# Retention into GLU on one core: one store issued from ScalarE, one gelu moved behind a value projection, operand splits given other predecessors

## The chip, the cores and the metric

The kernel runs on one core of a Trainium2 chip. The metric is the device time of one execution in microseconds, as a median over runs. TensorE (PE) does the matrix products, VectorE (DVE), ScalarE (ACT) and GpSimd (POOL) the elementwise work, and transfers are issued from SyncE's queue (SP) and from ScalarE's queue.

## What is computed

The program is a two-layer trunk over 1024 frames of width 1024, in float32. Only layer 0 matters here, and of it the join of two branches:

```python
# branch A: state-space layer, then a gated linear unit
y = jax.nn.gelu(y)
y = y * jax.nn.sigmoid(y @ glu_w + glu_b)          # (1024 x 1024) @ (1024 x 1024)
# branch B: retention, 8 heads, in chunks
scores = einsum('bnihd,bnjhd->bnhij', q, k) * intra   # the mask
out = scores @ v + cross                               # then a norm per head
# join
x = x + concat([y * silu(g_s5), out * silu(g_ret)]) @ w_out
```

Layer 1 (projections, a causal convolution of width 31, a norm and an output projection) follows and is the same in both kernels.

## The kernel before

**Products.** Every float32 weight and operand is split into a high and a low part (`h`, `l` in tile names: `wh_`/`wl_` for weights, `y11h`/`y11l` for operands), and each product is three matmuls of 512 columns: L200 (high by high), L201 (weight high by operand low), L202 (weight low by operand high). A weight block of 512 KB is loaded from SP into one of three `wf` buffers, ACT makes the high part (L189), and POOL or DVE the low part (L190).

**Stages.** Layer 0 runs the input projections beside the state-space layer, then `retention` with four pairs of heads (0 to 3), then the gated linear unit (GLU), then the output projection `mm_wo`. In each pair TensorE projects k (`mm_k`), q (`mm_q`) and the values (`mm_v`, eight blocks of 128 frames, each copied out by ACT at L1115 as `v`). Then it transposes k (`ktp`), makes the states (`kv`, summed by DVE into `S` at L1185), the scores (`sp`) and the outputs (`ro`). The scores are copied and masked by DVE into `sc` (L1198), twice for each half of the frames; `self.masked[0]` and `self.masked[1]` are the last of these for each half. The outputs are normalised (BN_STATS L1235, `rs` L475 on ACT, `on` L1241), turned (`rt`, L1249) and multiplied with the gate (`grl`, L1252).

**The GLU's operand.** While retention runs, `y_pass(k)` makes the operand of the GLU from y (rows k and k+4 of eight blocks). It loads y into `yp`, applies gelu on ACT (L958, tiles `yn_0` to `yn_7`), stores the result to DRAM (`yn_d`, L960), and then has DVE combine the two tiles in place (L966 to L969; the first of them overwrites half of the second tile and so needs its store done). The combinations are split (`th` L973, low part L974) and stored (`t_d`). The `yp` buffer is single: the two loads and the two `th` tiles of a pair use it in turn, so the second `th` needs the first one's store done.

**The GLU.** Its product is done with seven quarter-size products in place of eight. The first two quarters of y, `y11` and `y21`, come from `yn_d` by `load_split`: a load into a `wf` buffer (SP, L1284), a high part on ACT (L1260), a low part on DVE (L1262). The quarter products are `mm_glu1x` (x = 0 to 3: weight blocks `glu0` with `y11` and `glu1` with `y21` for x = 0 and 1, `glu2` and `glu3` for x = 2 and 3), then `mm_glu6x` (operand `yt2`, weights `glu4` and `glu5`) and so on. Their PSUM buffers are three in rotation: `mm_glu13` takes the one that `mm_glu10` had, once ACT has read it by the tanh `sg0` (L1337), and that stands behind the last `rs` of retention.

**What sets the order.** The program is handed to a scheduler that orders each engine's instructions by priorities and a simulated time line; each engine then runs its own list in order. `tc.issue_after(ins)` tells it not to place an instruction before another. `load_split` has two such hooks, `cast` for the high parts and `behind` for the low parts:

```python
def split(self, src, hi, lo, eng, behind=None, cast=None):
    with self.tc.issue_after(cast.ins) if cast else nullcontext():
        self.nc.scalar.copy(hi[:], src)
    with self.tc.issue_after(behind.ins) if behind else nullcontext():
        return eng.tensor_tensor(lo[:], src, hi[:].bitcast(F32), op=ALU.subtract)
```

`self.third_v` is the copy of the third value block of a pair and `self.last_v` that of the eighth. `self.last_kt` is the last copy of the transposed keys (L1158).

Of the kernel before, what the change touches and what calls it, by code (L numbers as in the profile page):

```python
# [19 lines left out]
P = 128  # L20
# [21 lines left out]
def mv(ap):  # L42

    return ap.rearrange("p (a c) -> p c a", a=LANES)


def un(ap):

    return ap.rearrange("p (c a) -> p a c", a=LANES)


def nat(ap):

    return ap.rearrange("p (a c) -> p a c", a=LANES)
# [16 lines left out]
class Trunk:  # L71
# [875 lines left out]
    def y_pass(self, rp, k):  # L947


        nc = self.nc  # L950
        yns = []
        for i, cb in enumerate((k, k + 4)):
            yt = rp.tile([P, 8, P], F32, name=f"yp_{cb}", tag="yp", bufs=1)
            nc.sync.dma_start(yt[:], self.y_d[cb].rearrange("i h g m -> (h g) i m"))
            yn = rp.tile([P, P, 8], F32, name=f"yn_{cb}", tag="ynt", bufs=2)

            with self.tc.issue_after((self.last_v if i else self.third_v).ins) if k == 2 else nullcontext():
                nc.scalar.activation(yn[:], yt[:].rearrange("p i m -> p m i"), AF.Gelu_apprx_tanh)  # L958
            yn = yn[:].rearrange("p m i -> p (m i)")
            nc.sync.dma_start(self.yn_d[cb * P:(cb + 1) * P], yn)  # L960
            yns.append(yn)
        (b11, b12), (b21, b22) = ((y[:, :HALF], y[:, HALF:]) for y in yns)
        v = nc.vector
        yield
        with self.tc.issue_after(self.last_raw.ins):
            v.tensor_tensor(b22, b22, b12, op=ALU.subtract)  # L966
            v.tensor_tensor(b12, b12, b11, op=ALU.subtract)
            v.tensor_tensor(b11, b22, b11, op=ALU.add)
            v.tensor_tensor(b21, b11, b21, op=ALU.subtract)  # L969
        yield  # L970
        for i in range(2):
            hi = rp.tile([P, T], F32R, name=f"th{i}_{k}", tag="yp", bufs=1)
            v.tensor_copy(hi[:], yns[i])  # L973
            v.tensor_tensor(yns[i].bitcast(F32R), yns[i], hi[:].bitcast(F32), op=ALU.subtract)  # L974
            nc.sync.dma_start(self.t_d[i, 0, k * P:(k + 1) * P], hi[:].bitcast(F32))
            nc.sync.dma_start(self.t_d[i, 1, k * P:(k + 1) * P], yns[i])
# [121 lines left out]
    def ret_values(self, pair):  # L1098

        nc = self.nc  # L1100
        wv = [self.wnext(f"v{pair}_{i}") for i in range(2)]
        vt = self.rp.tile([P, 8, 256], F32, name=f"v_{pair}", tag="v", bufs=2)
        for b in range(8):
            ps = self.bank(f"mm_v{pair}_{b}", aux=False)
            h, o = b // 4, (b % 4) * P
            for kb in range(KB):
                xh, xl = self.xs[h][kb]
                i, k4 = kb // 4, kb % 4
                wh = wv[i][0][:].rearrange("p (k a) n -> p k (a n)", a=2)[:, k4, :]
                wl = wv[i][1][:].rearrange("p (k a) n -> p k (a n)", a=2)[:, k4, :]  # L1110
                wh, wl = mv(wh), mv(wl)
                nc.tensor.matmul(ps[:, :256], xh[:, o:o + P], wh, start=kb == 0, stop=False)
                nc.tensor.matmul(ps[:, :256], xh[:, o:o + P], wl, start=False, stop=False)
                nc.tensor.matmul(ps[:, :256], xl[:, o:o + P], wh, start=False, stop=kb == KB - 1)
            self.last_v = nc.scalar.mul(nat(vt[:, b, :]), un(ps[:, :256]), self.Rtok[:, b:b + 1])  # L1115
            if b == 2:
                self.third_v = self.last_v
        return lambda p, b, hh: vt[:, b, hh * P:(hh + 1) * P]

    def ret_values_wide(self):  # L1120
# [143 lines left out]
    def layer0_back_and_layer1(self, st):  # L1264
        nc, A = self.nc, self.A
# [8 lines left out]
        def load_split(parts, name, h, wide, behind=None, cast=None):  # L1274

            res = []
            for i, part in enumerate(parts):
                if wide:
                    if i % 2 == 0:
                        f2 = self.wp.tile([P, 2, HALF], F32, name=f"{name}f{i}", tag="wf", bufs=3)  # L1280
                    f = f2[:, i % 2, :]
                else:
                    f = lp.tile([P, HALF], F32, name=f"{name}f{i}", tag="tp", bufs=3)[:]
                nc.sync.dma_start(f, part)  # L1284
                a, b = (self.op_tile(self.opA, f"A{h}", f"{name}{q}{i}") for q in "hl")
                self.split(f, a, b, v, behind, cast)
                res.append((a, b))
            return res
# [5 lines left out]
        B = lambda j, h: [self.yn_d[rows(4 * j + k), hs(h)] for k in range(4)]  # L1294
# [8 lines left out]
                res.append(ops)  # L1303
            return res

        b11, b21 = load_split(B(0, 0), "y11", 0, True, None, self.last_v), load_split(B(1, 0), "y21", 0, True, self.last_kt, self.last_v)
        ys = [[None] * KB for _ in range(2)]

        u2 = [lp.tile([P, HALF], F32, name=f"gu2_{n}", tag=tag, bufs=1) for n, tag in enumerate(("cq", "cs", "pilot", "sq"))]
# [618 lines left out]
```

## Time and profile before

| | us |
|---|---|
| median of 3 runs | 1147.6 (1144.61 to 1149.13) |
| span of the profiled execution | 1149.0 |
| PE busy | 1125.3 (98%) |
| DVE busy | 847.4 (74%) |
| POOL busy | 654.3 (57%) |
| ACT busy | 489.5 (43%) |
| mean granted TensorE clock | 0.991 |

The page gives the profiled execution's span and no other time of it; the span lies among the three runs. Matmuls overlap, and a busy PE in this table is not a PE at its peak. TensorE stands still for about 24 us in all, and an instruction of any engine waits for the ones ahead of it in the same engine's list.

### The profile page before, as it was taken

Reading aid. Unit: us, or ns where it says so; the run is one execution under the profiler, and the core shown is the slowest. Engines: PE = TensorE matmul, PEld = TensorE weight load, DVE = VectorE, ACT = ScalarE, POOL = GpSimd, SP = SyncE. Lnnn points to the kernel's source line nnn. Section 1 sums busy time; section 2 is a strip of 40 time slices with the busy share of each in tenths; the row PEclk is TensorE's granted clock in tenths of the full one; section 3 lists DMA queues with packets and bytes.
Section 4 is the critical chain, followed back from the end, with each engine's and each line's share of the span. In section 5 each row is a group of like instructions: output and inputs, shape, how many; then the busy total and the mean of one; then the engine's idle time right before and its main releaser. Section 6 shows DMA issues by size and latency. Waiting matters only on the chain.

```text
span 1149.0 us, 17198 instructions
## 1 busy us (share of the span) xinstructions
PE 1125.3 (98%) x6286; PEld 986.1 (86%) x6286; DVE 847.4 (74%) x1464; ACT 489.5 (43%) x719; POOL 654.3 (57%) x448
## 2 busy tenths in 40 slices
PE   9999999999999999989899999999999999999997
PEld 7888878888888889889788888888888888888787
DVE  6975788887418469484669622599999889999844
ACT  6423222333223231322446523555545677444674
POOL 2059999999246354232476011489544568677663
PEclk9999999999999999989899999999999999999999
DMA  9344445556388766858999988665778755357865
GB/s 352 111 134 154 122 164 177 179 174 206 114 279 290 241 220 186 292 171 304 348 382 308 342 287 282 185 240 202 239 256 293 242 188 175 119 182 257 287 226 193
DMA packets 117636, 261.45 MB, mean 228 GB/s; under 512 B 10672, under 2 KB 42288, under 8 KB 116912
## 3 DMA queue, kind: packets, MB, share of 16 engines
q1 hardware_dynamic: 114096, 247.78, 64.1%
q10 hardware_dynamic: 3456, 12.58, 2.9%
q8 instruction: 49, 0.80, 0.3%
q14 instruction: 35, 0.29, 0.1%
HBM read 181.48 MB, written 74.65 MB: 223 GB/s over the span
## 4 chain that ended last, share of the span: by engine, by line
PE 74%; DVE 13%; DMA 5%; issue 3%; POOL 3%; ACT 2%; SPq 0%; POOLq 0%; DVEq 0%; ACTq 0%
DVE cv L1535 5%; PE mm_wo L201 5%; PE mm_wo L200 5%; PE mm_wo L202 5%; PE mm_g L200 4%; PE mm_g L201 4%; PE mm_g L202 4%; PE mm_b L201 2%; PE mm_b L202 2%; PE mm_b L200 2%; PE mm_a L202 2%; PE mm_a L201 2%; PE mm_a L200 2%; PE mm_u L202 2%; PE mm_u L200 2%
## 5 line engine op out<-in xcount | busy, mean ns | idle before, releaser
L1535 DVE SCALAR_TENSOR_TENSOR cv<-u,convw,cv 128x512 f32<-128x512 f32 x398 | 273.0, 748 | 6.8 <-ACT cv L1514 4.8
L1508 POOL TENSOR_TENSOR tp<-tp,tp 128x512 f32<-128x512 f32 x64 | 82.9, 1296 | 33.9 <-ACT tp L1507 32.8
L200 PE MATMUL mm_g<-xh,wh_g 128*128 128x512 f32 x256 | 99.4, 388 | 0.0
L201 PE MATMUL mm_g<-xl,wh_g 128*128 128x512 f32 x256 | 98.1, 383 | 0.0
L202 PE MATMUL mm_g<-xh,wl_g 128*128 128x512 f32 x256 | 97.9, 382 | 0.0
L437 POOL TENSOR_TENSOR s1q<-s1q,s1q 128x512 f32<-128x512 f32 x12 | 17.1, 1427 | 81.4 <-ACT s1q L432 81.4
L1507 ACT ACTIVATE tp<-u,convw 128x512 f32<-128x512 f32 x64 | 45.4, 719 | 35.6 <-POOL tp L1508 34.8
L200 PEld LDWEIGHTS mm_g<-xh,wh_g 128*128 128x128 f32 x256 | 48.8, 191 | 8.7 <-issue 1.2
L202 PEld LDWEIGHTS mm_g<-xh,wl_g 128*128 128x128 f32 x256 | 48.8, 191 | 7.1
L201 PEld LDWEIGHTS mm_g<-xl,wh_g 128*128 128x128 f32 x256 | 48.7, 190 | 6.9 <-issue 0.4
L190 POOL TENSOR_TENSOR wl_v<-wf_v,wh_v 128x1024 fp32r<-128x1024 f32 x12 | 31.0, 2590 | 38.0 <-ACT wh_v L189 38.0
L190 POOL TENSOR_TENSOR wl_glu<-wf_glu,wh_glu 128x1024 fp32r<-128x1024 f32 x14 | 35.1, 2506 | 30.7 <-ACT wh_glu L189 30.7
L202 PE MATMUL mm_oc<-zh,wl_woc 128*128 128x512 f32 (+1 forms) x144 | 51.0, 357 | 0.3 <-DMA wl_woc<-lo_woc 0.3
L201 PE MATMUL mm_oc<-zl,wh_woc 128*128 128x512 f32 (+1 forms) x144 | 51.1, 356 | 0.0
L200 PE MATMUL mm_oc<-zh,wh_woc 128*128 128x512 f32 (+1 forms) x144 | 50.7, 363 | 0.0
L201 PE MATMUL mm_u<-xl,wh_u 128*128 128x512 f32 x128 | 48.5, 381 | 0.7 <-DVE xl L316 0.7
L200 PE MATMUL mm_wo<-ysh,wh_wos 128*128 128x512 f32 x128 | 48.9, 382 | 0.0
L200 PE MATMUL mm_g<-h1h,wh_cg 128*128 128x512 f32 x128 | 48.9, 382 | 0.0
L201 PE MATMUL mm_b<-h1l,wh_cb 128*128 128x512 f32 x128 | 48.7, 381 | 0.1
L202 PE MATMUL mm_b<-h1h,wl_cb 128*128 128x512 f32 x128 | 48.6, 380 | 0.0
L201 PE MATMUL mm_wo<-ysl,wh_wos 128*128 128x512 f32 x128 | 48.5, 379 | 0.0
L202 PE MATMUL mm_wo<-ysh,wl_wos 128*128 128x512 f32 x128 | 48.5, 379 | 0.0
(526 smaller groups left out, 3613.3 us busy)
## 6 DMA issues: line engine op xcount, KB each, us to landing
wf_g<-w_ab SPq DMA_DIRECT2D x16, 512.0 KB
wf_wos<-w_out SPq DMA_DIRECT2D x16, 512.0 KB
wf_wor<-w_out SPq DMA_DIRECT2D x16, 512.0 KB
wf_cb<-w_c SPq DMA_DIRECT2D x16, 512.0 KB
wf_ca<-w_c SPq DMA_DIRECT2D x16, 512.0 KB
wf_woc<-w_out_c SPq DMA_DIRECT2D x16, 512.0 KB
wf_v<-w_v SPq DMA_DIRECT2D x12, 512.0 KB
wf_cg<-w_c SPq DMA_DIRECT2D x11, 512.0 KB
```

What stands on the lines that cost most here:

```text
L190: self.low_made = lo[i].tensor_tensor(wl[:].rearrange(fl)[:, c], wf[:, c], h.bitcast(F32), op=ALU.subtract)
L200: nc.tensor.matmul(ps, wh[:, kb, :], xh, start=start, stop=False, **more)
L201: nc.tensor.matmul(ps, wh[:, kb, :], xl, start=False, stop=False, **more)
L202: self.last_mm = nc.tensor.matmul(ps, wl[:, kb, :], xh, start=False, stop=stop, **more)
L437: nc.gpsimd.tensor_tensor(a, a, sq[:], op=ALU.add)
L1507: nc.scalar.mul(sk[:], u[:, k:k + HALF], cw[:, nb, k:k + 1])
L1508: gp.tensor_tensor(s0[:], s0[:], sk[:], op=ALU.add)
L1535: v.scalar_tensor_tensor(dst[:], *tap, accs_[i][:], op0=ALU.mult, op1=ALU.add)
```

## The change

Four edits, all at the end of retention:

1. The store of `yn_6` (pair 2, second tile) is issued from ACT's queue in place of SP's.
2. The gelu of `yn_7` (pair 3, second tile) is placed behind the third value block of pair 3.
3. The high parts of `y11` are placed behind the sixth value block of pair 3 in place of the eighth.
4. The low parts of `y21` are placed behind the last masks of pair 3 in place of the last copy of the transposed keys.

```diff
-            with self.tc.issue_after((self.last_v if i else self.third_v).ins) if k == 2 else nullcontext():
+            behind = {(2, 0): self.third_v, (2, 1): self.last_v, (3, 1): self.third_v}.get((k, i)) if k > 1 else None
+            with self.tc.issue_after(behind.ins) if behind else nullcontext():
                 nc.scalar.activation(yn[:], yt[:].rearrange("p i m -> p m i"), AF.Gelu_apprx_tanh)
             yn = yn[:].rearrange("p m i -> p (m i)")
-            nc.sync.dma_start(self.yn_d[cb * P:(cb + 1) * P], yn)
+            (nc.scalar if (k, i) == (2, 1) else nc.sync).dma_start(self.yn_d[cb * P:(cb + 1) * P], yn)
...
             if b == 2:
                 self.third_v = self.last_v
+            elif b == 5:
+                self.late_v = self.last_v
...
-        b11, b21 = load_split(B(0, 0), "y11", 0, True, None, self.last_v), load_split(B(1, 0), "y21", 0, True, self.last_kt, self.last_v)
+        b11, b21 = load_split(B(0, 0), "y11", 0, True, None, self.late_v), load_split(B(1, 0), "y21", 0, True, self.masked[1], self.last_v)
```

No instruction is added or removed. Every engine's list is the same up to the end of pair 2's values and again from the first few blocks of `mm_wo` on; between them the scheduler moved more than the four edits name. In the changed kernel a line of the functions below `y_pass` has a number one to three higher.

ACT, at the end of pair 2's values (`rs_4` is pair 2's first norm). Before:

```order
L958 ACTIVATE yn_6_4620<-yp_6_4618 128x1024
L189 CAST wh_v3_0_4843<-wf_v3_0_4842 128x1024
L475 ACT_TABLE_LOAD
L475 ACTIVATE rs_4_0_4720<-mv_4_0_4711,epst_78 128x4
L475 ACTIVATE rs_5_0_4738<-mv_5_0_4729,epst_78 128x4
```

Now:

```order
L959 ACTIVATE yn_6_4620<-yp_6_4618 128x1024
L189 CAST wh_v3_0_4843<-wf_v3_0_4842 128x1024
L961 DMA yn_d_89<-yn_6_4620 128x1024
L475 ACT_TABLE_LOAD
L475 ACTIVATE rs_4_0_4720<-mv_4_0_4711,epst_78 128x4
```

The store now stands on ACT behind the gelu and one cast. On SP it stood behind the two loads of the gate (`grl_4`, `grl_5`) and ahead of two weight loads, which all stay there.

DVE, around the masks of pair 3. Before:

```order
L1262 TENSOR_TENSOR y21l0_5471<-y21f0_5468,y21h0_5470 128x512
L1185 SCALAR_TENSOR_TENSOR S_3_5246<-S_3_5246,g128_3202,kv1_3_5260 128x128
L1262 TENSOR_TENSOR y21l1_5476<-y21f0_5468,y21h1_5475 128x512
L1185 SCALAR_TENSOR_TENSOR S_3_5246<-S_3_5246,g128_3202,kv1_3_5260 128x128 x2
L1262 TENSOR_TENSOR y21l2_5482<-y21f2_5479,y21h2_5481 128x512
L1262 TENSOR_TENSOR y21l3_5487<-y21f2_5479,y21h3_5486 128x512
L1198 TENSOR_TENSOR sc0_3_5270<-sp10_3_5284,retmask_3_4836 128x512
L1198 TENSOR_TENSOR sc1_3_5271<-sp11_3_5285,retmask_3_4836 128x512
L1235 BN_STATS st_6_0_5316<-ro0_6_5300 128x6 x4
```

Now:

```order
L1188 SCALAR_TENSOR_TENSOR S_3_5246<-S_3_5246,g128_3202,kv1_3_5260 128x128
L1201 TENSOR_TENSOR sc1_3_5271<-sp01_3_5273,retmask_3_4836 128x512
L1201 TENSOR_TENSOR sc0_3_5270<-sp10_3_5284,retmask_3_4836 128x512
L1201 TENSOR_TENSOR sc1_3_5271<-sp11_3_5285,retmask_3_4836 128x512
L1265 TENSOR_TENSOR y21l0_5471<-y21f0_5468,y21h0_5470 128x512
L1265 TENSOR_TENSOR y21l1_5476<-y21f0_5468,y21h1_5475 128x512
L1265 TENSOR_TENSOR y21l2_5482<-y21f2_5479,y21h2_5481 128x512
L1265 TENSOR_TENSOR y21l3_5487<-y21f2_5479,y21h3_5486 128x512
L1238 BN_STATS st_6_0_5316<-ro0_6_5300 128x6 x4
```

The states and masks no longer have the low parts of `y21` between them; the low parts now stand ahead of retention's statistics.

ACT and SP, at the GLU's first operands and weights. ACT before:

```order
L1260 CAST y21h0_5470<-y21f0_5468 128x512
L1260 CAST y21h1_5475<-y21f0_5468 128x512
L1260 CAST y21h2_5481<-y21f2_5479 128x512
L1364 COPY gu2_0_5490<-mm_glu10_5498 128x512
L1260 CAST y21h3_5486<-y21f2_5479 128x512
L1364 COPY gu2_1_5491<-mm_glu11_5499 128x512
L189 CAST wh_glu2_5501<-wf_glu2_5500 128x1024
```

ACT now:

```order
L1263 CAST y21h0_5470<-y21f0_5468 128x512
L1367 COPY gu2_0_5490<-mm_glu10_5498 128x512
L189 CAST wh_glu2_5501<-wf_glu2_5500 128x1024
L1367 COPY gu2_1_5491<-mm_glu11_5499 128x512
L1263 CAST y21h1_5475<-y21f0_5468 128x512
L1263 CAST y21h2_5481<-y21f2_5479 128x512
L1263 CAST y21h3_5486<-y21f2_5479 128x512
```

Three of the four high parts of `y21` now stand behind the cast of the weight block `glu2`. SP now, from the store of `yn_7` on (`x2` is two loads):

```order
L1212 DMA grl_6_5296<-gr_d_88 128x1024
L1212 DMA grl_7_5298<-gr_d_88 128x1024
L961 DMA yn_d_89<-yn_7_5210 128x1024
L976 DMA t_d_91<-th0_3_5217 128x1024
L977 DMA t_d_91<-yn_3_5205 128x1024
L1287 DMA y21f0_5468<-yn_d_89 128x512 x2
L1305 DMA yt2h0_5506<-t_d_91 128x512
L976 DMA t_d_91<-th1_3_5222 128x1024
L1287 DMA y21f2_5479<-yn_d_89 128x512 x2
```

Before, the store of `yn_7` stood ahead of the swap of q (`qswp`), and the loads of `y21` behind all eight loads of `yt2` and two of `yt3`. Between this piece and the load of `wf_glu3` there now stand, besides those before, the loads `y22f` (3), `convw` and `xr` (2), which before came after it. On TensorE, 21 of the 24 matmuls of `y11` with `glu0` now stand ahead of pair 3's `kv`; before, two did.

## The prediction

> **What bounds the kernel now.** I read TensorE's own waits first, because the program is one long train of matmuls, and then the time line of each engine around them. In the stretch the change touches (470 to 600 us) the waits are three (us in total, times, longest):
>
> ```profile
> PE ro L1221 <- DVE sc L1198: 6.8, 2, 4.5
> PE ro L1221 <- DVE S L1185: 1.9, 1, 1.9
> PE mm_glu L200 <- ACT y11h L1260: 0.2, 1, 0.2
> ```
>
> Two stalls, then, both at the outputs `ro`, both for DVE's masks. TensorE's time line (start, duration, idle time before) shows the first in pair 2 and the second in pair 3:
>
> ```profile
> 484.87 2.05 PE L1226 MATMUL ro<-v,sc 128*128 128x128 f32 x16
> 486.85 0.48 PE L1221 MATMUL ro<-S,qrot 64*128 64x128 f32 x2
> 491.82 2.07 PE L1221 MATMUL ro<-S,qrot 64*128 64x128 f32 x14 [4.49 <-DVE sc L1198]
> 493.83 3.41 PE L1226 MATMUL ro<-v,sc 128*128 128x128 f32 x16
> 497.00 0.46 PE L200 MATMUL mm_k<-xh,wh_k 128*128 128x512 f32 x1
> ...
> 534.51 1.04 PE L1156 MATMUL ktp<-ident,krot 128*128 128x128 f32 x8
> ...
> 552.83 2.07 PE L1221 MATMUL ro<-S,qrot 64*128 64x128 f32 x14 [2.32 <-DVE sc L1198]
> 554.83 3.62 PE L1226 MATMUL ro<-v,sc 128*128 128x128 f32 x16
> 558.21 0.46 PE L200 MATMUL mm_glu<-y21h,wh_glu 128*128 128x512 f32 x1
> ...
> 577.53 0.38 PE L202 MATMUL mm_glu<-y21h,wl_glu 128*128 128x512 f32 x1
> ```
>
> A stall costs more than its idle time: the 16 products with `v` take 2.0 us up to the next start at 484.87 and 3.2 us at 493.83, after the stall. The granted clock (the number ahead of the last two) tells why, and that not every stall does this (rows: window in us, its length, busy time and count of PE, PEld, DVE, ACT and POOL, clock, DMA share, GB/s):
>
> ```profile
> 160.00:162.00 2.00, 0.79 (x4) 0.74 (x5) 2.00 (x4) 0.00 (x0) 1.92 (x2) 1.00 0.00 0
> 162.00:164.00 2.00, 2.00 (x7) 1.54 (x7) 2.00 (x3) 0.00 (x0) 2.00 (x3) 0.55 0.00 0
> ...
> 1076.00:1078.00 2.00, 0.00 (x0) 0.00 (x0) 1.90 (x4) 0.37 (x1) 0.25 (x1) 1.00 0.47 184
> 1078.00:1080.00 2.00, 1.62 (x3) 0.59 (x4) 2.00 (x4) 2.00 (x4) 0.72 (x1) 1.00 0.97 309
> ```
>
> After 160 us the clock is near half (right behind the second stall it is 0.73, in a row further down); after 1076, with a whole window idle, it stays at 1.00. At full clock the 14 + 16 `ro` matmuls need 2.07/2 + 1.98 = 3.0 us; they took 5.2 (to 497.00) and 5.4 (to 558.21).
>
> **Edit 1, the store from ACT's queue.** What DVE waits for in pair 2 is the store of `yn_6`:
>
> ```profile
> 477.00 2.02 ACT L958 ACTIVATE yn<-yp 128x1024 f32<-128x1024 f32 x1 [3.84 <-DMA yp<-y_d]
> 478.92 1.03 ACT L189 CAST wh_v<-wf_v 128x1024 fp32r<-128x1024 f32 x1
> ...
> 479.43 1.55 SPq L1209 DMA_DIRECT2D grl<-gr_d  x2
> 481.08 0.38 SPq L960 DMA_DIRECT2D yn_d<-yn  x1
> ...
> 487.61 0.69 DVE L966 TENSOR_TENSOR yn<-yn,yn 128x512 f32<-128x512 f32 x1 [4.76 <-DMA yn_d<-yn]
> 491.09 1.27 DVE L1198 TENSOR_TENSOR sc<-sp,retmask 128x512 f32<-128x512 f32 x2
> ...
> 517.45 0.32 SPq L960 DMA_DIRECT2D yn_d<-yn  x1
> ...
> 520.62 0.74 DVE L966 TENSOR_TENSOR yn<-yn,yn 128x512 f32<-128x512 f32 x1 [4.04 <-DMA yn_d<-yn]
> ```
>
> The gelu is done at 479.02, the store is issued at 481.08 behind two gate loads of 512 KB, and DVE goes on at 487.61, 6.53 us after the issue. The same store of `yn_7`, with no such loads ahead, took 3.17 us. DVE's in-order list has the second masks behind this step, and TensorE resumes 4.21 us after it. From ACT the store is issued when the cast ends, at about 480.0. Bounds for DVE's start: 483.1, if it lands as the lone store did, and 486.5, if only the 1.1 us of earlier issue is saved. I take 484.5: the lone store plus 1.3 us, the time of 512 KB at 0.39 MB/us (the saturated rate below), for sharing with one gate load. TensorE then resumes at 488.7 in place of 491.8, after 1.4 us of idle time. I take it that so short a stall leaves the clock up, which saves 5.2 - 3.0 = 2.2 us more: 3.1 + 2.2 = 5.3 us. The issue itself costs ACT next to nothing, since its next work, the norms, comes 15 us later.
>
> The Trainium skill (DMA: Bandwidth & Descriptors, Issuing engines are not separate DMA queues) speaks against this: it says that transfers from all queues run on the same DMA engines, and that issuing from another engine only saves the sequencer's issue time. By that the edit is worth the 1.1 us of the upper bound; this is the second rival. No row here shows a store from ACT's queue beside loads.
>
> **Edit 2, the late gelu.** It now runs behind the third value copy, and its store stands behind `grl_6` and `grl_7` on SP:
>
> ```profile
> 521.31 0.47 ACT L1115 ACTIVATE v<-mm_v,Rtok 128x256 f32<-128x256 f32 x1 [2.21 <-PE mm_v L1114]
> ...
> 531.81 0.69 DVE L973 CAST th<-yn 128x1024 fp32r<-128x1024 f32 x1 [6.41 <-DMA t_d<-th]
> 532.54 1.23 DVE L974 TENSOR_TENSOR yn<-yn,th 128x1024 fp32r<-128x1024 f32 x1
> 535.15 1.29 DVE L1158 TENSOR_TENSOR kt<-ktp,kdec 128x512 f32<-128x512 f32 x2 [1.38 <-PE ktp L1156]
> 537.99 1.88 DVE L1262 TENSOR_TENSOR y11l<-y11f,y11h 128x512 fp32r<-128x512 f32 x3
> ```
>
> With 5.3 us gained, the copy starts at 516.0 and the gelu ends at 518.5. The store lands 3.17 to 6.53 us later; I take 523, between them. DVE then has four combinations (2.9), `th` and its low part (0.69, 1.23), three low parts of `y11` (1.88), the second `th`, whose buffer is free 3.17 us after the first one's store is issued (529.8), a low part of `y11` and one of `yn_7`, and `kt`, done at 533.6. TensorE asks for `kt` at 534.5: `ktp` ends at 530.0 (529.2 + 0.8), and the 21 `y11` matmuls that edit 3 puts ahead take 4.5 (0.2165 us each: 462 in the 100 us of a row below). So edits 2 and 3 cost nothing; a store at 525.0 would cost 1.1 us. The swap of q and the gate stores gain by leaving this store's shadow on SP, and nothing waits for them.
>
> **Edit 4, the low parts behind the masks.** In pair 3 the masks waited for `y21`, whose load came late:
>
> ```profile
> 547.13 1.29 ACT L1260 CAST y21h<-y21f 128x512 fp32r<-128x512 f32 x2 [9.88 <-DMA y21f<-yn_d]
> ...
> 552.10 1.28 DVE L1198 TENSOR_TENSOR sc<-sp,retmask 128x512 f32<-128x512 f32 x2
> ```
>
> Now they don't. From `ktp` to the first `y21` matmul, 23.7 us pass; less 4.4 of waits and 2.4 of half clock that is 16.9 us of work. TensorE is ready for `y21` at 529.2 + 16.9 = 546.1, 12.1 us earlier than before. It can't keep this, because the new lists hang the next steps on transfers:
>
> ```profile
> 534.54 2.38 POOL L190 TENSOR_TENSOR wl_glu<-wf_glu,wh_glu 128x1024 fp32r<-128x1024 f32 x1 [5.88 <-ACT wh_glu L189]
> ...
> 552.54 1.05 ACT L189 CAST wh_glu<-wf_glu 128x1024 fp32r<-128x1024 f32 x1 [0.59 <-DMA wf_glu<-w_glu]
> 553.29 0.88 DVE L1235 BATCH_NORM_STATS2 st<-ro 128x6 f32<-128x128 f32 x4
> 563.02 1.40 ACT L1337 ACTIVATE sg<-mm_glu,hgb 128x512 f32<-128x512 f32 x2
> ...
> 536.00:540.00 4.00, 4.00 (x51) 3.32 (x51) 4.00 (x8) 1.25 (x3) 0.91 (x1) 1.00 0.77 247
> 556.00:560.00 4.00, 4.00 (x21) 3.81 (x20) 4.00 (x19) 0.00 (x0) 0.01 (x1) 0.73 1.04 390
> ```
>
> The load of `y21` takes the buffer of `glu1`, free when POOL's low part ends: 536.9 - 5.3 = 531.6. SP waits for that with everything behind it. From there to `wf_glu2` SP's new list has 3.93 MB (sizes by tile shape). A transfer's fixed part is 3.17 - 1.34 = 1.8 us; at 0.39 MB/us `wf_glu2` lands at 543.5, at 0.247 at 549.3. I take 545, nearer to the saturated row, since here too many transfers are queued. The high parts of `y21` now stand behind its cast: cast 1.05, copy 0.5, three high parts 1.9, a low part 0.7, so the last low part is done at 549.1, and only then come retention's statistics. From the statistics to the end of the first tanh took 10.4 us, of which a cast that has moved was 1.0; so the tanh ends at 558.5. `mm_glu13` needs the PSUM buffer that it reads. TensorE gets there earlier: the last `y21` operand plus 27 matmuls and `mm_glu12`'s turn (0.8) is 555.8. **The new stall is there, 2.7 us**, and may halve the clock again; I take that it does, since the two stalls nearest in place did. The 12 matmuls take 5.2 us in place of 2.6 and end at 563.7. `wf_glu3` has moved behind 1.4 MB more; 5.9 MB after `wf_glu2` it lands at 560.1, its low part is ready at 563.5, and is hidden. Four matmuls and eight turns (1.7) and then 22 matmuls (4.8) end the `y21` products at 570.2. Before, they ended at 577.7 with eight other matmuls (1.7) among them: 576.0. **Sum: 5.8 us.** Behind this TensorE has no gaps to speak of, and the later lists are alike:
>
> ```profile
> 600.00:700.00 100.00, 99.67 (x462) 86.98 (x461) 59.65 (x75) 45.98 (x66) 28.20 (x17) 1.00 0.89 308
> 800.00:900.00 100.00, 99.87 (x460) 86.46 (x459) 99.46 (x150) 53.17 (x76) 50.81 (x38) 1.00 0.77 262
> ```
>
> So the whole rest moves up. Against the profiled span of 1149.0 that is 1143.2; the span is 1.4 over the median of the runs, and 1147.6 - 5.8 = 1141.8.
>
> **Rivals.** *The clock stays up in the new stall* (0.15): the idle window at 1076 speaks for it, the one at 160 against. `mm_glu13` ends at 561.1, the low part of `glu3` at 563.5 decides, and the products end at 568.3: 7.7 us, 1139.9; with a store at 483.1 1.3 more, 1138.6. The Trainium skill (TensorE: Matmul & The Clock Gate, What's actually happening) has the clock drop after an idle window of some 3.4 us; by that neither of my stalls would halve it. The trace does not agree throughout: at 160 some 2 us sufficed.
>
> *The store gains its issue time alone* (0.27): TensorE stalls 3.4 us in pair 2, the clock still halves, edit 1 is worth 1.1, and the chain from `wl_glu1` on is 4.2 later: 1.6 to 3.5 us gained, 1144 to 1146. The 6.53 us behind queued loads speak for it, if a store from another queue shares their fate.
>
> *Slower* (0.07): the transfers starve TensorE at `glu3`. Before, SP had 8.4 MB from the same point up to `wf_glu3`; now 9.8 MB. Equal time needs `wf_glu3` at 567.8, that is 9.83 MB in 34.4 us: below 0.286 MB/us the change loses. At the 0.247 of the slow row it lands at 573.2, and the time is 1153.0. The saturated rows speak against that.
>
> *The gain is lost later* (0.08): DVE is 99% busy from 800 to 900 us, and were its convolution not started by TensorE's results, nothing would be left, 1147.6. It is started by them.
>
> **How the numbers follow.** The forecast has 0.37, and mixtures of the cases the remaining 0.06. The range, 1138.0 to 1147.5, runs from the best case to no change. 0.5% (5.7 us) is about what a measurement can tell from no change, and my forecast lies on that line: half of it, the first rival and a part of the mixtures make 0.40 faster, the starved case most of the 0.06 slower, and 0.54 is the same.
>
> **What would show it.** Right: DVE's first combination of pair 2 near 484.5 and a clock of 1.00 behind it; no wait of `ro` for `sc` in pair 3; a new wait of `mm_glu` for ACT's tanh near 556; `y21h` split in two by a cast that waits for `wf_glu`. Wrong: that combination at 486 or later, a late `kt`, or a wait of TensorE for `wl_glu3`, which would make the queue the bound.

## The result, and the profile after

The changed kernel takes 1144.1 us (median of 22 runs, 1139.5 to 1148.0), the kernel before 1147.2 us beside it (median of 22, 1142.8 to 1152.2). The ratio is 0.9976, with an interval of 0.9965 to 0.9987: 3.1 us, or 0.24%, faster. That is within the 0.5% called no change, above the forecast of 1141.8 us and inside its range. Of the runs used below one, of the kernel with both stores on ACT, took 2010.2 us at a mean clock of 0.612, against 1141 to 1149 us for its others, and its ratio leaves that run out.

The profiled execution of the changed kernel has a span of 1140.0 us and took 1142.0 us, 2.2 below its median. The one of before has a span of 1149.0; runs of that kernel take 1.8 us more than their span, so it took 1150.8, and lies 3.6 above its median. The two profiles differ by 9.0 us, and the runs by 3.1.

TensorE's waits of the changed kernel, from 470 to 640 us (us in total, times, longest):

```profile
PE mm_glu L200 <- ACT sg L1340: 1.7, 1, 1.7
PE mm_glu L201 <- DVE y11l L1265: 1.0, 2, 0.7
PE mm_glu L201 <- DVE y21l L1265: 0.9, 1, 0.9
PE rt L1252 <- DVE on L1244: 0.5, 1, 0.5
```

Both stalls of `ro` for the masks, 6.8 us before, are gone, and so is the one for `S`. The largest wait is a new one, of `mm_glu` for ACT's tanh. In pair 2 ACT, SP, DVE and TensorE now read (start, duration):

```profile
474.51 2.00 ACT L959 ACTIVATE yn<-yp 128x1024 f32<-128x1024 f32 x1 [3.28 <-DMA yp<-y_d]
...
476.54 0.33 ACTq L961 DMA_DIRECT2D yn_d<-yn  x1
...
476.94 1.55 SPq L1212 DMA_DIRECT2D grl<-gr_d  x2
...
481.05 0.69 DVE L967 TENSOR_TENSOR yn<-yn,yn 128x512 f32<-128x512 f32 x1
...
484.54 1.27 DVE L1201 TENSOR_TENSOR sc<-sp,retmask 128x512 f32<-128x512 f32 x2
...
484.92 1.51 PE L1224 MATMUL ro<-S,qrot 64*128 64x128 f32 x16
486.36 2.05 PE L1229 MATMUL ro<-v,sc 128*128 128x128 f32 x16
488.17 0.46 PE L200 MATMUL mm_k<-xh,wh_k 128*128 128x512 f32 x1
```

The store is issued as the gelu ends, ahead of both gate loads. DVE starts on `yn_6` at 481.05 without any wait, 4.5 us after the issue at most. The 16 and 16 `ro` matmuls run in one piece, in 3.25 us. The list has a cast between the gelu and the store, but the store's issue did not wait for that cast, which ran from 476.42 to 477.45. Everything here stands 1.9 us earlier than before, for reasons that are not the change's. At 160 us this execution wins 2.9 us: TensorE stood still for 1.0 us there and not for 2.0, and the 15 matmuls behind it ran at full clock (3.4 us up to the next products, against 5.1 with the clock halved on the way). It loses 1.0 us in the stretch called "values" below. In before's time (times of this profile plus 1.9) DVE starts at 483.0. The new stall, and the clock behind it:

```profile
552.89 1.06 PE L1252 MATMUL rt<-ident,on 128*128 128x128 f32 x8 [0.50 <-DVE on L1244]
...
555.68 0.48 PE L200 MATMUL mm_glu<-y11h,wh_glu 128*128 128x512 f32 x1 [1.72 <-ACT sg L1340]
```

```profile
552.00:556.00 4.00, 1.78 (x11) 1.16 (x10) 3.19 (x18) 2.90 (x5) 0.00 (x0) 1.00 1.05 394
556.00:560.00 4.00, 4.00 (x24) 3.48 (x22) 3.46 (x8) 3.37 (x5) 2.08 (x1) 1.00 1.03 394
```

The granted clock (the third number from the end) stays at 1.00, and the DMA engines are full (the next number, 1.05 and 1.03).

To compare executions I cut TensorE's time line at five places, each cut at the first matmul of a kind, in us. "Values" is from pair 2's fourth block of q to its `ktp`, "pair 2" from there to pair 3's last keys, "pair 3" from pair 3's `ktp` to the first `mm_wo`; the piece between pair 2 and pair 3 takes 37.5 to 38.0 in all. Ahead of these stretches the profiles differ by up to 4.2 us, around the stall at 160 us, and behind them by up to 1.8.

| kernel | values | pair 2 | pair 3 |
|---|---|---|---|
| before | 26.7 | 24.5 | 90.9 |
| before, repeated | 27.2 | 21.8 | 90.6 |
| changed | 27.7 | 17.6 | 89.2 |
| changed, repeated | 31.0 | 17.4 | 90.6 |
| store only | 31.0 | 17.4 | 90.1 |
| change without the store | 27.5 | 21.8 | 89.4 |

### The profile page after: what moved, and what is told of

It reads as the page before. It is cut to its first block, busy times and chain, and to the rows that moved or that the text cites. A ratio compares the mean times of both kernels' runs of the same rounds, so it can differ in the third digit from the quotient of the medians.

```text
span 1140.0 us, 17201 instructions
## 1 busy us (share of the span) xinstructions
PE 1120.9 (98%) x6286; PEld 980.3 (86%) x6286; DVE 863.7 (76%) x1464; ACT 489.4 (43%) x719; POOL 659.4 (58%) x448
## 4 chain that ended last, share of the span: by engine, by line
PE 69%; DVE 19%; DMA 4%; ACT 2%; issue 2%; POOL 2%; SPq 0%; POOLq 0%; DVEq 0%; ACTq 0%
DVE cv L1538 11%; PE mm_wo L201 5%; PE mm_wo L200 5%; PE mm_wo L202 5%; PE mm_g L200 4%; PE mm_g L201 4%; PE mm_g L202 4%; PE mm_u L202 2%; PE mm_u L200 2%; PE mm_u L201 2%; PE mm_oc L202 2%; PE mm_glu L202 2%; PE mm_oc L201 2%; PE mm_glu L200 1%; PE mm_oc L200 1%
```

## The experiments

The theory after the result: edit 1 brings nearly all, because the store no longer stands behind the gate loads; edits 2 and 3 cost nothing and edit 4 trades pair 3's stall for the one at the tanh. The rivals: the gain is in edits 2 to 4; or the profiles differ by chance, and the edits do little.

**The store alone, and the change without it.** The first is the kernel before with edit 1, the second the changed kernel without it:

```diff
-            nc.sync.dma_start(self.yn_d[cb * P:(cb + 1) * P], yn)
+            (nc.scalar if (k, i) == (2, 1) else nc.sync).dma_start(self.yn_d[cb * P:(cb + 1) * P], yn)
```

```diff
-            (nc.scalar if (k, i) == (2, 1) else nc.sync).dma_start(self.yn_d[cb * P:(cb + 1) * P], yn)
+            nc.sync.dma_start(self.yn_d[cb * P:(cb + 1) * P], yn)
```

> Edit 1 alone: only the store of yn_6 goes out from ACT's queue; the late gelu, the casts and the low parts of y stay as before. My theory, from the two profiles: the stretch from pair 2's first transposed keys (ktp) to the first key product of pair 3 behind the ro products, 24.5 us before and 17.6 after, is all the store's: 17.5 to 18.5 us here, no wait of ro for sc in pair 2, the clock at 1.00. The stall of pair 3 is back (4.2 us of waits or more, half clock), since its masks still stand behind the low parts of y21. In time 5 to 7 us below before, by the profiles. First rival, that the profiled run of before was an unlucky one and its stall is shorter in most runs: the stretch is the same 17.5 to 18.5, but the runs gain only 1 to 3 us. Second rival, the store gains its issue time alone: the stretch is 21 us or longer.

> The whole change without edit 1: the store of yn_6 is again issued on SP, behind the two gate loads. My theory: the stall of pair 2 is back (the stretch from ktp to pair 3's key products is 23 to 25 us), pair 3's masks wait for nothing, and the stretch from pair 3's ktp to the first mm_wo takes 88 to 90 us against 90.9 before and 89.2 after; in time 0 to 3 us below before. Rival, that edits 2 to 4 lose what the store gains and so the runs show 3 us where the profiles show 9: slower than before by 1 to 4 us, with a wait of TensorE for a weight of the gates or for kt in the trace.

Measured: the store alone 1144.8 us (0.9983, 0.9966 to 1.0001), the change without it 1147.1 (1.0011, 0.9993 to 1.0029), before on the same chip 1146.6. The store alone gains 1.8 us, with an interval that just reaches no change, where the theory had 5 to 7 and its first rival 1 to 3. It makes the whole gain of pair 2 (17.4 us, as in the changed kernel). Without it pair 2 takes the 21.8 us of before's second profile, and the runs gain nothing. From the time lines of the change without the store (first piece), and of the store alone (second piece):

```profile
475.71 0.38 SPq L961 DMA_DIRECT2D yn_d<-yn  x1
...
484.00 0.69 DVE L967 TENSOR_TENSOR yn<-yn,yn 128x512 f32<-128x512 f32 x1 [2.91 <-DMA yn_d<-yn]
...
488.22 1.16 PE L1224 MATMUL ro<-S,qrot 64*128 64x128 f32 x14 [2.65 <-DVE sc L1201]
```

```profile
474.00 1.52 SPq L1209 DMA_DIRECT2D grl<-gr_d  x2
...
476.44 0.33 ACTq L960 DMA_DIRECT2D yn_d<-yn  x1
...
484.08 0.68 DVE L966 TENSOR_TENSOR yn<-yn,yn 128x512 f32<-128x512 f32 x1
```

Without the store's edit the gelu ended at 473.7, the store was issued 2.0 us later behind the gate loads, landed 8.3 us after that, and `ro` waited 2.65 us. With it, the store was issued 0.04 us after its gelu, and DVE, busy with the states, did not wait for it, though here the gate loads had been issued first. By the records of queue q10 its last packet ended 6.1 us after the issue, and in the changed kernel 4.0 us after it. The DMA queues of the store-alone kernel from 480.0 to 480.5 us (packets, MB, share of the engines; q1 carries SP's transfers, q10 ACT's store):

```profile
q10 hardware_dynamic: 28, 0.11, 55.6%
q1 hardware_dynamic: 27, 0.10, 50.8%
```

In this half microsecond each queue has half of the engines, though SP's held transfers that were issued earlier. The Trainium skill (DMA: Bandwidth & Descriptors, Queues, rings and completion order) says that an engine goes round its queues packet by packet, and the rows agree. The even share is that of this stretch: in the half microsecond before it, q10 had 23.9% and q1 61.1%.

**Both kernels repeated**, without an edit, to see by how much one execution differs from the next.

> The changed kernel, profiled a second time, since its first profile is 9 us below that of before while the runs differ by 3. My theory: the two stretches at the change repeat to 0.5 us (17.6 from pair 2's ktp to pair 3's key products, 37.5 to pair 3's ktp, 89.2 to the first mm_wo), and what differs between executions lies elsewhere, at the kt products near 160 us and at the end. Rival, the new stall of mm_glu13 halves the clock in most executions and did not in the first profile: the last stretch is 91 to 93 us here.

> The kernel before, profiled a second time. My theory: 24.5, 37.5 and 90.9 us in the three stretches again, within 0.5. Rival, the profiled run of before was an unlucky one: the store lands sooner in this execution, DVE's combination starts less than 5 us behind the issue, and the first stretch is 19 to 22 us; or the masks of pair 3 come sooner and the last is under 89.5.

Measured: 1145.6 us for the changed kernel, 1147.6 for before. The pair 2 column above has 24.5 and 21.8 for the same program. In both the store was issued 2.1 us after its gelu, and DVE went on 6.5 and 6.3 us after the issue; but in the first profile the gelu had waited 3.8 us for its load, and 2.5 here, and so ended 1.4 us later against TensorE (6.5 and 5.2 us behind pair 2's `ktp`). So `ro` waited 4.5 us for the masks there and 2.9 here, and the clock from 480 to 500 us was 0.83 and 0.91. The first profile is not the odd one in this: the two variants of before that follow have 24.5 and 24.6 us in pair 2, and every profile with the store on ACT has 17.4 to 17.6. The changed kernel lost 3.4 us in the values column, and its new stall looked like this (one row of the time line, then two windows of 2 us):

```profile
557.63 0.79 PE L200 MATMUL mm_glu<-y11h,wh_glu 128*128 128x512 f32 x1 [1.72 <-ACT sg L1340]
```

```profile
556.00:558.00 2.00, 0.37 (x1) 0.37 (x2) 1.32 (x5) 1.99 (x3) 0.00 (x0) 0.82 0.65 216
558.00:560.00 2.00, 2.00 (x6) 1.55 (x6) 2.00 (x6) 0.63 (x2) 0.00 (x0) 0.50 0.88 334
```

The same stall of 1.72 us at the same instruction halved the clock here and left it at 1.00 in the other execution. Five profiles below and above have it, and the clock halved in two of them. The loss in the values column is this (DVE and POOL, changed kernel repeated; then the changed kernel):

```profile
446.34 3.16 DVE L975 TENSOR_TENSOR yn<-yn,th 128x1024 fp32r<-128x1024 f32 x1
446.06 2.36 POOL L190 TENSOR_TENSOR wl_k<-wf_k,wh_k 128x1024 fp32r<-128x1024 f32 x1 [2.55 <-ACT wh_k L189]
```

```profile
447.04 1.19 DVE L975 TENSOR_TENSOR yn<-yn,th 128x1024 fp32r<-128x1024 f32 x1
447.38 3.07 POOL L190 TENSOR_TENSOR wl_k<-wf_k,wh_k 128x1024 fp32r<-128x1024 f32 x1 [1.47 <-ACT wh_k L189]
```

In the first pair POOL starts first, DVE's low part of 1.2 us takes 3.2, and TensorE's `rt` then waits 2.9 us for the norm's statistics. In the second DVE starts first, POOL's takes 3.1 in place of 2.4, and the longest wait of TensorE that follows is 0.5. The Trainium skill (SBUF — State Buffer, SBUF: two separate sides) calls the port that DVE and GpSimd share an exclusive lock, held by whoever starts first for a whole instruction; the four rows agree. The store-alone profile had the same loss, with the same 2.9 us.

**POOL's low part later, in both kernels.** If that toss decides the runs, taking it away changes the gain:

```diff
-            self.low_made = lo[i].tensor_tensor(wl[:].rearrange(fl)[:, c], wf[:, c], h.bitcast(F32), op=ALU.subtract)
+            with self.tc.issue_after(self.last_turn.ins) if name == "k3" else nullcontext(): self.low_made = lo[i].tensor_tensor(wl[:].rearrange(fl)[:, c], wf[:, c], h.bitcast(F32), op=ALU.subtract)
```

> Before, with one more edit: POOL makes the low part of pair 3's key weight behind its last product of pair 2's swapped queries, in place of ahead of the second half of the turned queries. Two of six profiles so far (both with the store on ACT) have a stall of TensorE of 2.9 us ahead of pair 2's values, where DVE's low part of y took 3.2 us because POOL's low part of that weight had started 0.2 to 0.3 us ahead of it; in the four others DVE started first and took 1.2. My theory: this is a toss of each execution, worth 3.5 us, and independent of the change; here it can't fall, so the stretch from the last mm_q of pair 2 to its ktp is 27 to 28 us, no wait of rt for mv, and the time 0 to 2 us below before. Rival, the toss belongs to the store on ACT alone and before never has it: no difference in time (0 +- 1 us).

> The changed kernel with the same edit on POOL. My theory: the changed kernel loses the toss more often than before, and that is why its runs show 3 us of gain where the stretches at the change itself add up to 5 to 6; with the toss taken out the time is 4.5 to 6.5 us below before, and the stretch from the last mm_q to ktp is 27 to 28 us. Rival, the toss has nothing to do with it: the gain stays at 3 us (2 to 4).

Measured: before with it 1148.0 us (1.0017, 1.0000 to 1.0034), the change with it 1144.45 (0.9985, 0.9967 to 1.0002), before 1146.8. The two differ by 3.5 us, as before and change do without the edit (3.1), where the theory had 4.5 to 6.5 against before. The toss is real and costs 3.4 us where it is lost, but it doesn't make or hide the change's gain.

**The toss forced against DVE, in both kernels**, with `th` of pair 1's second tile made by a multiplication by ones, to start the low part half a microsecond later. The low part is held behind the four `on` that it followed before:

```diff
-            v.tensor_copy(hi[:], yns[i])
+            v.tensor_scalar(hi[:], yns[i], self.ones[:, 0:1], None, op0=ALU.mult) if (k, i) == (1, 1) else v.tensor_copy(hi[:], yns[i])
-            v.tensor_tensor(yns[i].bitcast(F32R), yns[i], hi[:].bitcast(F32), op=ALU.subtract)
+            with self.tc.issue_after(self.on_made.ins) if (k, i) == (1, 1) else nullcontext(): v.tensor_tensor(yns[i].bitcast(F32R), yns[i], hi[:].bitcast(F32), op=ALU.subtract)
...
```

> Before, with DVE half a microsecond late on purpose in pair 1: the copy th of the second y is made by a multiplication by a column of ones, which leaves the values as they are and takes some 1.2 us in place of 0.65; the order of the instructions stays (one transposition of PE apart). So POOL's low part of the key weight starts ahead of DVE's low part of y. My theory on why the runs gain less than the stretches: an execution in which POOL comes first loses 3.5 us ahead of pair 2's values, and in before it gets them back, because the store of yn_6 is then not late for TensorE; so in before the toss costs nothing. Here the stretch from the last mm_q to ktp is 30 to 31 us, that from ktp to pair 3's key products 17.4 to 19.5 in place of 21.8 to 24.5, and the time is before's, within 1.5 us. Rival, the two stalls add: 30 to 31 and then 21.8 or more, and the time is 3 to 4 us over before's.

> The changed kernel with the same late DVE. My theory: 30 to 31 us in the stretch ahead of ktp and 17.4 behind it, nothing to get back: 1 to 2.5 us over the changed kernel's median, which holds executions of both kinds (1145 to 1146.5), and only 0 to 2 us below before with the same late DVE. Rival, the stalls add in before: then the gain against the late before is the full 5 to 6 us.

Measured: 1147.0 us (0.9995, 0.9974 to 1.0016) and 1142.9 (0.9970, 0.9953 to 0.9986), before 1147.6. The multiplication took 0.98 us, as the copy in its place did, so nothing was forced: DVE's low part took 1.2 us in both, and the experiment does not test the toss. The pair is a third measurement of the gain, 4.1 us.

**The tanh's cast later.** The cast of `glu2` is placed behind the casts of `y21`, on top of the later low part:

```diff
-            nc.scalar.copy(h, wf[:, c])
+            with self.tc.issue_after(self.last_cast.ins) if name == "glu2" else nullcontext(): nc.scalar.copy(h, wf[:, c])
...
-            self.nc.scalar.copy(hi[:], src)
+            self.last_cast = self.nc.scalar.copy(hi[:], src)
```

> The same, and on ACT the cast of the third gate weight (wh_glu2) moved behind the casts y21h1 to y21h3 in place of ahead of them; nothing else moves on any engine. My theory: these casts waited for the cast, and that for wf_glu2's landing at 541; without it they run at about 536, the low parts behind the masks end 3 us sooner, the waits of mm_glu for y21l (0.9 to 1.6 us) vanish and that for the tanh (1.7) shrinks to below 0.5: 1.5 to 3 us off the stretch from pair 3's ktp to the first mm_wo. Rival, the wait for the tanh is set by DVE's statistics and the three table loads of ACT, or the weight's low part comes late: only 0 to 1 us is gained.

Measured: 1144.1 us (0.9974, 0.9955 to 0.9994), against 1144.45 without this edit. Its waits:

```profile
PE mm_glu L200 <- ACT wh_glu L189: 3.8, 1, 3.8
PE mm_glu L201 <- DVE y11l L1265: 1.7, 2, 1.5
...
PE mm_glu L200 <- ACT sg L1340: 0.3, 1, 0.3
```

The new stall goes from 1.7 to 0.3 us, and one of 3.8 for the weight block `glu3` takes its place. Pair 3 takes 91.2 us, longer than before's, where the theory had it 1.5 to 3 us shorter. The load had been late all along: in the changed kernel the cast runs at 556.8, hidden behind the tanh. The stall of 3.8 us left the clock at 1.00.

**Both stores of the second tiles from ACT**, on top of that:

```diff
-            (nc.scalar if (k, i) == (2, 1) else nc.sync).dma_start(self.yn_d[cb * P:(cb + 1) * P], yn)
+            (nc.scalar if (k, i) in ((2, 1), (3, 1)) else nc.sync).dma_start(self.yn_d[cb * P:(cb + 1) * P], yn)
```

> The same, and the store of yn_7 goes out from ACT's queue too; its issue stands right behind its gelu on either queue, so the issue time is the same, and only the queue differs. In the profiles of the changed kernel DVE goes on 5.3 us after the issue on SP, behind two loads of y11 and two gate loads. My theory (what the store gains is its place among the queued transfers): 3 to 4.5 us from issue to DVE's first combination, and the waits for y11l (1.0 us) vanish: 0.5 to 1 us. Rival, only the issue time counts: 5.3 us again, nothing gained.

Measured: 1143.6 us (0.9968, 0.9949 to 0.9986). The store of `yn_7`, from ACT (first two rows), and from SP in the changed kernel:

```profile
514.97 0.33 ACTq L961 DMA_DIRECT2D yn_d<-yn  x1
520.45 0.69 DVE L967 TENSOR_TENSOR yn<-yn,yn 128x512 f32<-128x512 f32 x1 [11.79 <-issue]
```

```profile
514.89 0.32 SPq L961 DMA_DIRECT2D yn_d<-yn  x1
520.22 0.69 DVE L967 TENSOR_TENSOR yn<-yn,yn 128x512 f32<-128x512 f32 x1 [11.61 <-issue]
```

5.5 and 5.3 us from issue to use, where the theory had 3 to 4.5: where nothing holds the issue up, the other queue gains nothing. By the rule of the Trainium skill that the prediction weighs (DMA: Bandwidth & Descriptors, Issuing engines are not separate DMA queues) that is so, and here the trace agrees. In pair 2 the issue was held up, for some 2 us. In this profile `glu3` is waited for again, 3.4 us, and here the clock halves (0.50 from 558 to 560 us).

**The change without edit 4**, to see what it is worth:

```diff
-        b11, b21 = load_split(B(0, 0), "y11", 0, True, None, self.late_v), load_split(B(1, 0), "y21", 0, True, self.masked[1], self.last_v)
+        b11, b21 = load_split(B(0, 0), "y11", 0, True, None, self.late_v), load_split(B(1, 0), "y21", 0, True, self.last_kt, self.last_v)
```

> The changed kernel without edit 4: the low parts of y21 stand behind the last kt again, ahead of pair 3's masks; wf_glu3 is loaded ahead of y22 as before. My theory: the waits of ro for S and sc in pair 3 are back, 4 us of them and the half clock, the waits of mm_glu for y21l and the tanh go; the stretch from pair 3's ktp to the first mm_wo is 90.5 to 92 us against 89.2 to 90.6 with the edit, so edit 4 is worth 0.5 to 2 us; in time 0.5 to 2 us over the changed kernel's 1144.1. Rival, edit 4 costs what it gains, by the late wf_glu3: within 0.5 us of the changed kernel, or below it.

Measured: 1142.7 us (0.9970, 0.9949 to 0.9991), beside 1142.9 for the change with the multiplication on the same chip. Pair 3's stall, which the store alone had left in place (`ro` waited 2.28 us for `sc`), did not come back, against the theory. SP and DVE, first of this kernel, then of before:

```profile
525.91 1.03 SPq L1287 DMA_DIRECT2D y21f<-yn_d  x2
...
533.32 2.71 DVE L1265 TENSOR_TENSOR y21l<-y21f,y21h 128x512 fp32r<-128x512 f32 x4
...
538.98 1.88 DVE L1201 TENSOR_TENSOR sc<-sp,retmask 128x512 f32<-128x512 f32 x3
```

```profile
541.80 0.91 SPq L1284 DMA_DIRECT2D y21f<-yn_d  x2
```

The low parts still stand ahead of the masks, but their load is issued 15.9 us earlier, and they are done at 536.0, 2.9 us before the last three masks begin. Of the 15.9 us, 9.1 are that pair 3 itself begins earlier; against pair 3's `ktp` the load is issued 0.5 us behind it, and in before 7.3. In the store-alone kernel, whose pair 3 begins earlier too and whose stall stayed, it is 7.5. So it is edits 2 and 3 that remove this stall: with them the loads of `y21` go ahead of those of `yt2` on SP. Edit 4 is worth nothing that can be measured: without it the stall of 1.7 us at the tanh is gone too, and one of 2.1 us at a later tanh (`mm_glus`) is there in its place. Which of edits 2 and 3 moves the loads was not tried.

**The cast later and `glu3` loaded earlier**, on the changed kernel: the loads of `yt3`, of the gate products, `y22`, `convw` and `xr` go behind it on SP.

```diff
+            ld = nc.sync.dma_start(wf[:, c], src.rearrange(fl)[:, c]); self.glu3_load = ld if name == "glu3" else getattr(self, "glu3_load", None)
...
-                nc.sync.dma_start(f, part)
+                with self.tc.issue_after(self.glu3_load.ins) if name == "y22" else nullcontext(): nc.sync.dma_start(f, part)
...
```

> The candidate: the changed kernel with the cast of wh_glu2 behind those of y21 (as in the run that had the new stall of 3.8 us for wf_glu3), and on SP the loads of yt3, of the gates' factors, of y22, the convolution's weights and xT behind that of wf_glu3, which so leaves SP some 10 us earlier. My theory: wf_glu3 was late only for its place in SP's queue; the wait for wh_glu vanishes, and the stretch from pair 3's ktp to the first mm_wo falls to 86.5 to 88 us, 2 to 3 below the changed kernel's; 1141 to 1142.5 us in the runs. Rival, the transfers as such are the bound: what stood ahead of wf_glu3 is late next (yt2 or yt3 for the later products), and the time stays at 1143 to 1145.

Measured: 1142.6 us (0.9969, 0.9949 to 0.9989), no better than its neighbours. The wait for `glu3` is gone, and pair 3 measures 86.9 us. But 12 matmuls of the GLU, which stood ahead of the first `mm_wo`, now stand behind it, and at 0.2165 us each they are 2.6 us: like for like pair 3 takes 89.5, and nothing is gained. Its waits, and its windows from 540 to 600 us:

```profile
PE mm_glu L200 <- ACT ysh L1347: 3.2, 1, 3.2
PE mm_glu L202 <- POOL wl_glu L190: 1.3, 1, 1.3
```

```profile
540.00:560.00 20.00, 19.63 (x113) 17.30 (x112) 13.63 (x58) 10.47 (x15) 10.91 (x6) 1.00 1.03 371
560.00:580.00 20.00, 20.00 (x95) 17.51 (x94) 11.36 (x17) 7.55 (x11) 11.17 (x6) 1.00 1.04 387
580.00:600.00 20.00, 16.96 (x77) 13.96 (x75) 13.25 (x14) 9.68 (x14) 16.46 (x10) 1.00 1.01 362
```

Pair 3 as one window, of before, of the changed kernel and of this one (the first count is TensorE's matmuls):

```profile
534.51:625.39 90.88, 86.12 (x470) 75.18 (x469) 64.93 (x130) 44.62 (x68) 53.06 (x29) 0.96 0.95 342
525.68:614.83 89.15, 84.43 (x470) 71.91 (x469) 73.10 (x131) 41.60 (x63) 52.08 (x27) 1.00 0.99 358
525.02:611.91 86.89, 81.19 (x458) 70.03 (x457) 61.87 (x126) 39.35 (x60) 50.07 (x26) 1.00 1.00 354
```

TensorE stands still in it for 4.8, 4.7 and 5.7 us: the waits move and do not shrink. The DMA share is full throughout, but the 3.2 us for `ysh` end with DVE, which has low parts of `y22` and `yr0` ahead of that step. So it is not shown that the transfers bound this stretch. No version here beats the changed kernel by more than the runs can tell.

## Why the prediction was right or wrong

**The class and the direction were right**: faster, by less than 0.5%. The forecast gain of 5.8 us was 2.7 too large. The range reached from the best case to no change, so that the time lies in it says little for the sum.

**Edit 1: the mechanism was right.** DVE's start, in before's time, was 483.0, against a forecast of 484.5 and a lower bound of 483.1. The forecast had the issue wait for the cast ahead of it, until 480.0; it came at 478.5. No stall was left, where 1.4 us were forecast, and the clock stayed at 1.00. The forecast was 5.3 us; the profiles show 7.1 (17.4 us in pair 2 against 24.5, as in three of four profiles of before and its variants), or 4.4 against the repeated one and the change without the store. The second rival, 1.1 us, is out.

**Edits 2 and 3, called free, cost 1.0 us and brought pair 3's gain.** TensorE waited 1.0 us for `y11l`, since DVE's three low parts took longer beside POOL's `wl_glu`:

```profile
524.87 4.05 DVE L1265 TENSOR_TENSOR y11l<-y11f,y11h 128x512 fp32r<-128x512 f32 x3
525.71 2.67 POOL L190 TENSOR_TENSOR wl_glu<-wf_glu,wh_glu 128x1024 fp32r<-128x1024 f32 x1 [8.10 <-ACT wh_glu L189]
```

I had taken 1.88 us from before. The steps around it held, in before's time: DVE's start on `yn_7` at 522.2 (forecast 523), `kt` done at 534.4 (533.6).

**Edit 4: the places were right, the attribution wrong.** TensorE was ready for the low parts of `y21` at 545.4 (forecast 546.1), the cast of `glu2` began at 543.0 (545), at `mm_glu13` at 555.9 (555.8), and went on there at 557.6 (558.5) after 1.7 us (2.7). But the masks would have been free of `y21` without this edit. The step that failed is "Now they don't [wait for `y21`]" as a consequence of edit 4; the order of the loads on SP, which the front part shows, was the cause.

**The clock in the new stall** was forecast to halve, with the rival that it stays up. The first profile has the rival, and the repeat has the forecast. From the values of pair 2 to the first `mm_wo` the first profiles differ by 7.7 us, the rival's figure, and the repeated ones by 1.1, with the toss lost in the changed kernel; that the first pair agrees is luck. All the halvings in the records of the fourteen traces, but for the one at each program's end, last 3.41 or 6.83 us: where a stall lowers the clock, it is for one or two such periods, and whether it does is not a matter of its length alone (1.72 us did in two of five profiles, 3.8 us did not). The Trainium skill (TensorE: Matmul & The Clock Gate, What's actually happening) has the clock drop after an idle window of some 3.4 us, and has these windows run freely, whatever the kernel does. The traces agree with the period; that the whole window must be idle they do not bear out, since 1.72 us can be enough.

**The term that was mis-sized** is the price of the stalls in the runs. The sum priced them in one execution, and took that execution as 1.4 us above the median, by its span; with the 1.8 us around the span it was 3.6 above. The record of every run has its mean granted clock, and shows what kind of execution it was (runs of the kernel before beside all the experiments, and of the changed one):

| mean clock | before: runs, mean us | changed: runs, mean us |
|---|---|---|
| 0.989 to 0.991 | 16, 1150.8 | none |
| 0.992 to 0.993 | 30, 1147.8 | none |
| 0.994 to 0.995 | 38, 1145.4 | 1, 1148.0 |
| 0.996 | 6, 1143.6 | 9, 1145.6 |
| 0.997 to 0.998 | none | 12, 1142.6 |

The profile of before, at 0.991, belongs to the lowest 16 of 90. The mean over all runs is 0.9931, which is 2.4 us less of lost clock; the changed kernel's profile, at 0.998, lies 1.7 us on the other side of its mean of 0.9965. Together that is some 4 of the 5.9 us by which the profiles differ more than the runs. The other profiles are alike: the four profiled executions of before and its two variants lie 0.4 to 3.6 us above their medians, those of the changed kernel and its two variants between 2.2 below and 1.4 above. So prices read from before's time lines are too high for its runs.

What the gain in the runs consists of is not settled. Over all runs before loses 7.9 us to the clock (1 - 0.9931 of 1147.0), the changed kernel 4.0, and the difference, 3.9 us, is more than the whole gain of 3.0 in the means. Time multiplied by clock is 1139.2 us before and 1140.0 with the change, and at an equal clock of 0.996 the changed kernel is 2.0 us the slower (9 runs against 6). By this count the gain is all clock that is no longer halved, and the idle time that pair 2 saves (2.9 to 4.5 us) does not show up. But the count charges to the clock also halved time in which TensorE stands still, inside a stall and at the program's end: by the traces' records that is 2.2 to 3.6 us in the four profiles of before and its variants, and 0.6 to 1.7 in those of the changed kernel and its variants. Without it, if the runs are like the profiles in this, the clock's part of the gain is some 2 us by estimate. That leaves some 1 us of idle time, still less than pair 2 saves.

The half changes suggest where idle time is given back. On one chip time multiplied by clock is 1138.8 us for before (23 runs), 1137.9 for the store alone (12) and 1142.2 for the change without the store (12), whose mean clock is the higher one (0.9949, before 0.9933) and whose time is no shorter. So edits 2 to 4 seem to spare half clock and to cost other time, some 2 us with the same reserve, where the prediction put edits 2 and 3 at nothing. In pair 3 TensorE stands still for 4.8 us before and 4.7 with the change: the waits for the masks and for `S` were exchanged for others, and the stretch takes 90.2 to 90.9 us for before and its two variants, and 88.5 to 90.6 for the changed kernel and its two. The rest stays open: only the profiled executions have a time line. The toss at 447 us, which I took for the likeliest place, is not it, since the pair without it gains as much.

**The case of starvation** (0.07) was not seen in the changed kernel, but is next in line: one edit further TensorE waits 3.8 us for `glu3`.

## What to carry to other kernels

A store that others wait for should not stand behind loads in one in-order queue: what counted here is the moment of its issue, some 2 us earlier from another engine's queue; where the issue was free, the other queue gained nothing. Before a gain is summed from stalls, look at a second execution and at the granted clock of the runs: a sum made on one execution can promise too much, and an edit that removes a wait may put another as long in its place. When several edits are made together, look in each queue's order for the one that moves the loads, since the edit that is named after a wait need not be the one that removes it.

## What was not expected of the hardware

- A stall of 1.72 us at one instruction halved the clock in two profiled executions (0.50 behind it) and left it at 1.00 in three; one of 3.8 us left it at 1.00. The halvings last 3.41 or 6.83 us.
- DVE's low part of 128x1024 takes 1.2 or 3.2 us, and POOL's 2.4 or 3.1, as the one or the other starts first; starts that differed by some 0.6 us turned it and cost TensorE 2.9 us. In the changed kernel with the multiplication, where POOL's began 0.07 us ahead, DVE's took 1.2 all the same, and POOL's 3.5.
- A store of 512 KB needed 4.5 us at most when it was issued ahead of two loads of its size, and 6.3 to 8.3 us behind them in one queue.
